# The gated MLP of a hybrid decoder block: convolution accumulated in PSUM, weight splits on GpSimd, token combinations made before the transposes

## The chip, the cores and the metric

The kernel runs on one core of one Trainium2 chip. The metric is the device time of one execution in microseconds (us). Engines are named TensorE (PE in the profile, PEld for its weight loads), VectorE (DVE), ScalarE (ACT), GpSimd (POOL) and SyncE (SP, which only issues DMAs here). The inputs and the output are float32, and so are all intermediate values.

## The reference

One decoder block on 1024 tokens of width 1024. Two groups of attention heads (stick-breaking and latent attention) share an input projection and an output projection; after that comes the part that the change touches, and a gated per-layer embedding at the end:

```python
x = x + rms_norm(mix, g_post_mix[i])

h = rms_norm(x, g_pre_ffn[i])
u = causal_depthwise_conv(h @ w_up[i], conv_w[i], conv_b[i])   # w_up: 1024 x 5632, three taps
gate, val = jnp.split(u, 2, axis=-1)
f = (jax.nn.gelu(gate, approximate=True) * val) @ w_down[i]    # w_down: 2816 x 1024
x = x + rms_norm(f, g_post_ffn[i])
```

## The kernel before

**Float32 by three products.** TensorE multiplies float32r operands. Each float32 value is split into a high part h (a rounding copy on ScalarE, line 97) and the rest l = value − h (one subtraction, line 98, on VectorE or, with `on_pool`, on GpSimd). A product is then three matmuls: h·h, h·l and l·h. The split's source can be in SBUF or, on VectorE, in PSUM.

**The up projection by seven block products.** The 1024 x 5632 product is made in 22 channel groups c of 128 gate and 128 value columns. For each, the 2 x 2 blocks are: token half (first, second 512 tokens), half of the 1024 inputs (k4), and gate or value (v). Instead of eight block products it makes seven, with sums of weight blocks and sums of token blocks. Two of the seven (`up_first`, lines 959 to 978) need only the first token half and run as filler inside the attention and the output projection; their results go to DRAM (`p1_dram`, `u_dram`). The other five need the token tiles t1 to t4 and b22, which are built from both halves (`combined`), and the weight sums s[0] to s[3] and one plain block (`up_sums`, `up_sum_4`, lines 925 to 935). Each of the five is twelve matmuls of 128x512 (`up_product`, lines 915, 917 and 922).

**The loop over channels** (from line 1221). For each c the five products t2, t1, t3, t4, b22 go into two PSUM banks, py and pz. py gathers t2, t3 and t4, and VectorE reads it after each of them (lines 1237, 1240, 1243); pz gathers t1 and b22 and is read at lines 1241 and 1245. The sums u of gate and value (128 channels x 1024 tokens) then go through `conv`: ScalarE writes y = w2·u + b (line 1215), VectorE adds two shifted terms in place (line 1217, y is in SBUF), ScalarE applies gelu to the gate's y (line 1247), VectorE multiplies it by the value's y (line 1248), and GpSimd's queue stores the product to `f_dram` (line 1249). Six PSUM banks go round for the products. The weights of the following products are made alongside: SP loads raw blocks (line 1205, five buffers, `WR`), GpSimd makes the four sums (lines 928, 929, 930, 934), ScalarE the high parts, and the low parts of two of the five splits are made by VectorE and of three by GpSimd. The split weights lie in a ring of eight slots.

**The token tiles.** `out_proj_mla` (from line 765) finishes the output projection of one token half: it normalises, adds x (line 798, on GpSimd), stores the sum, normalises again (line 805), and transposes 128 x 128 blocks (line 809). For the first half (th = 0) the transposed rows are split into `h2`. For the second half (th = 1) `combined` (from line 816) works on transposed tiles: it rebuilds the first half's values from h + l on GpSimd (line 832), copies one block out of PSUM (line 839), makes t1, t2, t3 on VectorE (lines 837, 841, 843) and t4 on GpSimd (line 849), and splits the five results, two of them on GpSimd.

**Order.** Each engine runs its instructions in a fixed order. The order is made when the program is built, from the order of the code, given priorities, and a simulated timeline; filler work is handed out by credits (`Fill.step`): `WO_RATE` is the credit per step of the output projection (first number) and per step marked "sums" or "chain" (second number). Buffers are taken in turn, and an instruction waits until the buffer's last reader is done. After the loop comes the down projection (`ffn_down`, line 1294), which needs four banks at a time and the same raw buffers `wr`.

Of the kernel before, what the change touches and what calls it, by code (L numbers as in the profile page):

```python
# [37 lines left out]
ML_RATE = (1.2, 0.8)  # L38
WO_RATE = (0.3, 2.5)
AHEAD = 0.9  # L40
EMB_RATE = 1.0

WR = 5
LATER = (500, 0, 0, 2000)
# [6 lines left out]
def tile_hybrid_block(ctx: ExitStack, tc: tile.TileContext, a: dict, out: bass.AP):  # L51
# [149 lines left out]
    def bank():  # L201
        return now["bank"]()
# [567 lines left out]
    def out_proj_mla(th, rows, h2):  # L770
# [21 lines left out]
        for j, t in enumerate(ts):  # L792
            dve.scalar_tensor_tensor(rows[j], rows[j], r[:, j:j + 1], g_post_mix, ALU.mult,
                                     ALU.mult)
            for h_ in hd_:
                xt = tmp()
                sp.dma_start(xt, a["x"][t * P:(t + 1) * P, h_])
                pool.tensor_tensor(rows[j][:, h_], rows[j][:, h_], xt, ALU.add)
            pool.dma_start(x1_dram[t], rows[j])
            yield "chain"  # L800
        r = rstd_rows()
        for j in range(4):
            for k4, h_ in enumerate(hd_):
                n = tmp()
                dve.scalar_tensor_tensor(n, rows[j][:, h_], r[:, j:j + 1], g_pre_ffn[:, h_],
                                         ALU.mult, ALU.mult)
                ps = bank() if th == 0 else one_bank(ptr, "tr")
                for k in range(4):
                    pe.transpose(ps[:, k * P:(k + 1) * P], n[:, k * P:(k + 1) * P], ident)
                if th == 0:  # L810
                    d = [z[:, k4 * 4:k4 * 4 + 4, j * P:(j + 1) * P] for z in h2]
                    split(d[0], d[1], ps.rearrange("p (k t) -> p k t", k=4))
                    yield "chain"
                elif k4 == 0:
                    ps0 = ps
                else:
                    yield from combined(j, ps0, ps, *h2)

    def combined(j, b12, b22, first, ts_):


        def out(i, src, on_pool=False):
            d = [z[:, :, j * P:(j + 1) * P] for z in ts_[i]]
            split(d[0], d[1], src.rearrange("p (k t) -> p k t", k=4), None, on_pool)

        def tmp2():
            return now["wo"].tile([P, H], F32, tag="wh", name=nm("t"), bufs=4)

        def raw(k4):
            t = tmp2()  # L830
            d = [z[:, k4 * 4:k4 * 4 + 4, j * P:(j + 1) * P] for z in first]
            pool.tensor_tensor(t.rearrange("p (k t) -> p k t", k=4), d[0], d[1], ALU.add)
            return t

        b11 = raw(0)
        t1 = tmp()
        dve.tensor_tensor(t1, b12, b11, ALU.subtract)
        s22 = tmp()
        act.copy(s22, b22)
        t2 = tmp()  # L840
        dve.tensor_tensor(t2, s22, t1, ALU.subtract)
        t3 = tmp2()
        dve.tensor_tensor(t3, s22, b12, ALU.subtract)
        out("t1", t1, True)
        yield "chain"
        out("t3", t3)
        b21 = raw(1)
        t4 = tmp2()
        pool.tensor_tensor(t4, b21, t2, ALU.subtract)
# [75 lines left out]
    def up_sums(raw, s):  # L925

        a21, a22, a11 = (raw(1, 0), raw(1, 1), raw(0, 0))
        pool.tensor_tensor(s[0], a21, a22, ALU.add)
        pool.tensor_tensor(s[1], s[0], a11, ALU.subtract)
        pool.tensor_tensor(s[2], a11, a21, ALU.subtract)  # L930
        return (s[1], False), (s[0], False), (s[2], True), (a22, True)

    def up_sum_4(raw, s1, dst):
        pool.tensor_tensor(dst, raw(0, 1), s1, ALU.subtract)
        return ((dst, True),)

    def first_up_sums():
# [14 lines left out]
        def splits(slots):  # L952
            last = sh.tile([P, H], F32, tag="uf", name=nm("uf"), bufs=3)
            res = []
            for src, on_pool in some + up_sum_4(raw, s[1], last):
# [24 lines left out]
    with tc.tile_pool(name="mla", bufs=1, side="right", reuse_waits="tile") as ml:  # L980
# [163 lines left out]
        for z in (make_k(0), make_q(0), make_k(1)):  # L1144
            for _ in z:
# [5 lines left out]
                 for n in range(16)]  # L1151
# [4 lines left out]
    y_cm[0].__exit__(None, None, None)  # L1156
    px = ctx.enter_context(tc.tile_pool(name="px3", bufs=2, space=PSUM, reuse_waits="tile"))
    py = ctx.enter_context(tc.tile_pool(name="py3", bufs=2, space=PSUM, side="right",
                                        reuse_waits="tile"))

# [9 lines left out]
    with tc.tile_pool(name="wo", bufs=1, side="right", reuse_waits="tile") as wo_:  # L1170
        now["wo"] = wo_
        rows1 = [sh.tile([P, D], F32, tag="s4", name=nm("row"), bufs=4) for _ in range(4)]
        for r in out_proj_sb(1, rows1):
            fill.step(WO_RATE[r in ("sums", "chain")])
        for r in out_proj_mla(1, rows1, (h2[0], tb)):
# [4 lines left out]
    now["bank"] = cycle([lambda: one_bank(px, "mm"), lambda: one_bank(py, "mm"),  # L1180
                         lambda: one_bank(pav, "av"), lambda: one_bank(px, "mm"),
                         lambda: one_bank(py, "mm"), lambda: one_bank(ppj, "pj")])
    shared.__exit__(None, None, None)
# [5 lines left out]

    def up_split(src, on_pool):  # L1190
# [9 lines left out]
    def up_weights():  # L1200

        for c in range(1, NCH):
            def raw(v, k4):
                t = up_tile("wr", 512, WR)
                sp.dma_start(t.rearrange("p (a b) -> p a b", a=4), up_block(v, c, k4))
                return t

            s = [up_tile("s", 512, 4) for _ in range(4)]
            for src, on_pool in up_sums(raw, s) + up_sum_4(raw, s[1], s[3]):
                yield up_split(src, on_pool)  # L1210

    def conv(v, c, u):
        y = up_tile(f"y{v}", S, 2)
        ci = v * NCH + c
# [8 lines left out]
    for c in range(NCH):  # L1223
# [22 lines left out]
        y = [conv(v, c, u[v]) for v in range(2)]  # L1246
        act.activation(y[0], y[0], AF.Gelu_apprx_tanh)  # L1247
        dve.tensor_tensor(y[0], y[0], y[1], ALU.mult)
        pool.dma_start(f_dram[c], y[0])
    tp_cm.__exit__(None, None, None)  # L1250
# [205 lines left out]
```

## Time and profile before

| | us |
|---|---|
| median of 3 runs | 1593.34 (1591.44 to 1596.71) |
| the profiled execution | 1593.64 |
| its span | 1591.5 |
| TensorE busy | 1434.4 (90%) |
| VectorE busy | 1164.3 (73%) |
| ScalarE busy | 831.4 (52%) |
| GpSimd busy | 607.6 (38%) |

A stage table has, for each stretch of time, the length and then for each engine the busy time and in brackets the number of instructions, then the clock granted to TensorE as a share of full speed, the busy share of the DMA engines, and the GB/s moved. A row of a line's view names line, engine, operation, what it writes and reads, the count, then the shortest, median and longest duration in ns, the first and the last start in us, and the shapes. A row of the waits has who waited, for whom, the total in us, the times, and the longest. A timeline row has start and duration in us, engine, line, operation and count, and in square brackets the idle time before it and what ended it.

### The profile page before, as it was taken

What the parts mean: (1) busy time and instruction counts of PE and PEld (TensorE: products, weight loads), DVE (VectorE), ACT (ScalarE), POOL (GpSimd) and SP (SyncE); (2) the same over time, 40 slices, a digit from 0 to 9 for tenths busy, and PEclk for the clock granted to TensorE, in tenths of its full rate; (3) what the DMA queues carried; (4) which work ended last, traced back from release to release, by engine and by line L of the source; (5) the groups of instructions that cost most, each with busy time, mean ns of one, the idle gap of its engine ahead of it and who ended that gap; (6) DMA issues with size and microseconds to landing.
All of it is one profiled execution on the core that took longest, in us unless ns stands there. A gap on an engine that the chain in (4) does not pass through costs nothing. (4 is left out here: it accounts for less than half of the span.)

```text
span 1591.5 us, 20521 instructions
## 1 busy us (share of the span) xinstructions
PE 1434.4 (90%) x6768; PEld 1169.9 (74%) x6768; DVE 1164.3 (73%) x1869; ACT 831.4 (52%) x1575; POOL 607.6 (38%) x548
## 2 busy tenths in 40 slices
PE   5997998987899888899987599989998999999996
PEld 4977886775688776778865487777767788888875
DVE  4569477999767778733567599999999654874697
ACT  6366455776778566645434343344344444654542
POOL 7107100011344325112365899889893000000033
PEclk9999999998999999999998799999999999999998
DMA  6031210122544433346654344444444766675354
GB/s 197 22 100 52 95 41 14 40 75 103 157 138 159 122 113 119 120 153 197 202 175 161 101 143 133 137 141 133 147 129 135 275 201 188 229 232 179 126 184 160
DMA packets 128570, 219.90 MB, mean 138 GB/s; under 512 B 13376, under 2 KB 50144, under 8 KB 128464
## 3 DMA queue, kind: packets, MB, share of 16 engines
q1 hardware_dynamic: 111920, 161.58, 32.9%
q0 software_dynamic: 16544, 57.01, 9.7%
q8 instruction: 53, 0.87, 0.2%
q14 instruction: 53, 0.43, 0.1%
HBM read 165.33 MB, written 53.22 MB: 137 GB/s over the span
## 5 line engine op out<-in xcount | busy, mean ns | idle before, releaser
L1217 DVE SCALAR_TENSOR_TENSOR y<-u,c_conv_w,y 128x1023 f32<-128x1023 f32 x88 | 162.8, 1852 | 9.3 <-ACT y L1215 9.2
L98 DVE TENSOR_TENSOR tl<-tr,th 128x512 fp32r<-128x512 f32 x192 | 103.2, 549 | 40.4 <-ACT th L97 35.1
L97 ACT CAST th<-tr 128x512 fp32r<-128x512 f32 x192 | 90.9, 485 | 53.8 <-PE tr L464 44.2
L98 DVE TENSOR_TENSOR wl<-ws,wh 128x512 fp32r<-128x512 f32 x73 | 63.5, 879 | 70.1 <-ACT wh L97 33.2
L464 PE MATMUL tr<-ident,w 128*128 128x128 f32 x576 | 103.2, 287 | 10.1 <-DVE tl L98 6.0
L98 DVE TENSOR_TENSOR f<-wr,f 128x512 fp32r<-128x512 f32 x88 | 60.7, 690 | 68.5 <-PE pj L122 34.3
L1215 ACT ACTIVATE y<-u,c_conv_b,c_conv_w 128x1024 f32<-128x1024 f32 x44 | 54.8, 1245 | 89.7 <-DVE u L1245 53.1
L1292 POOL DMA_DIRECT2D x_dram<-fd x8 | 4.3, 541 | 246.6 <-DVE fd L1291 235.0
L652 DVE TENSOR_TENSOR_SCAN kc<-kc,one_f 128x128 f32<-128x128 f32 (+3 forms) x64 | 88.0, 1381 | 13.0 <-ACT kc L649 12.9
L464 PEld LDWEIGHTS tr<-ident,w 128*128 128x128 f32 x576 | 74.4, 147 | 25.7 <-DVE tl L98 7.7
L479 PE MATMUL av<-tl,v 128*128 128x512 f32 x192 | 76.6, 400 | 18.4 <-DVE tl L98 17.9
L478 PE MATMUL av<-th,v 128*128 128x512 f32 x192 | 78.5, 409 | 13.4 <-ACT th L97 7.0
L98 POOL TENSOR_TENSOR ws<-s,ws 128x512 fp32r<-128x512 f32 x42 | 88.9, 2121 | 3.0 <-ACT ws L97 3.0
L97 ACT CAST f<-wr 128x512 fp32r<-128x512 f32 x88 | 54.5, 619 | 68.1 <-PE pj L121 30.5
L120 PE MATMUL mm<-wh,f 128*128 128x512 f32 x220 | 85.9, 393 | 0.0
L121 PE MATMUL mm<-wl,f 128*128 128x512 f32 x220 | 85.5, 391 | 0.0
L97 ACT CAST wh<-ws 128x512 fp32r<-128x512 f32 x76 | 46.7, 620 | 74.3 <-DMA ws<-in_w_up 27.8
L97 ACT CAST wh<-wr 128x512 fp32r<-128x512 f32 x88 | 54.6, 621 | 49.4 <-DMA wr<-in_w_down 35.7
L98 DVE TENSOR_TENSOR wl<-wr,wh 128x512 fp32r<-128x512 f32 x88 | 63.1, 717 | 19.1 <-ACT wh L97 19.0
L122 PE MATMUL mm<-wh,f 128*128 128x512 f32 x220 | 74.1, 393 | 0.0
L748 POOL TENSOR_TENSOR t<-t,t 128x512 fp32r<-128x512 f32 x32 | 41.2, 1289 | 84.1 <-ACT t L747 41.2
L1247 ACT ACTIVATE y<-y 128x1024 f32<-128x1024 f32 x22 | 23.4, 1062 | 85.5 <-DVE y L1217 85.5
(518 smaller groups left out, 4724.1 us busy)
## 6 DMA issues: line engine op xcount, KB each, us to landing
wr<-in_w_down SPq DMA_DIRECT2D x88, 256.0 KB, 3.0
wr<-f_dram SPq DMA_DIRECT2D x88, 256.0 KB, 2.9
wr<-in_w_up SPq DMA_DIRECT2D x84, 256.0 KB, 2.8
t<-o_dram SPq DMA_DIRECT2D x48, 256.0 KB, 3.1
ws<-in_w_up SPq DMA_DIRECT2D x47, 256.0 KB, 3.5
f_dram<-y POOLq DMA_DIRECT2D x22, 512.0 KB, 3.6
ws<-in_w_o SPq DMA_DIRECT2D x32, 256.0 KB, 3.1
ws<-in_w_in SPq DMA_DIRECT2D x24, 256.0 KB, 2.9
```

The lines of the kernel that those rows point to most:

```text
L97: act.copy(h, src)
L98: (pool if on_pool else dve).tensor_tensor(l, src, h, ALU.subtract)
L120: pe.matmul(ps, lh, rh, start=start, stop=False)
L121: pe.matmul(ps, lh, rl, start=False, stop=False)
L122: pe.matmul(ps, ll, rh, start=False, stop=stop)
L464: pe.transpose(tr[:, c:c + P], w[i][:, j * P:(j + 1) * P], ident)
L478: pe.matmul(av[:, lo:], v(j), th[:, lo:], start=j == 0, stop=False)
L479: pe.matmul(av[:, lo:], v(j), tl[:, lo:], start=False, stop=j == last)
L652: dve.tensor_tensor_scan(rev, rev, one_f[:, 0:1].to_broadcast([P, n]), 1.0, ALU.mult, ALU.mult)
L748: pool.tensor_tensor(ol, src, oh, ALU.subtract)
L1215: act.activation(y, u, AF.Identity, bias=conv_b[:, ci:ci + 1], scale=conv_w[:, ci, 2:3])
L1217: dve.scalar_tensor_tensor(y[:, d:], u[:, :S - d], conv_w[:, ci, 2 - d:3 - d], y[:, d:], ALU.mult, ALU.add)
```

## The change

Four things change in the code.

1. `conv` puts y into four PSUM banks (two tiles of two banks, one buffer each) and no longer into SBUF; gelu writes a new SBUF tile f, which is multiplied in place by the value's y and stored. The product banks fall from six to four: the pools px and py are closed before the loop and opened again after it.
2. In the loop all five splits run with `on_pool`, that is, their low part on GpSimd. The four sums stay as they are. The splits of the first channel (`first_up_sums`) all run on VectorE.
3. `combined` works on rows before the transposes. The first half's normalised rows are stored to `n0_dram` and loaded again; t1 to t4 are made on VectorE from rows in SBUF, and each of the five results is transposed into a PSUM bank and split from there, on ScalarE and VectorE. The addition of x for the second half moves from GpSimd to VectorE.
4. `WR` goes from 5 to 6, the second `WO_RATE` from 2.5 to 1.8, and the first four banks of the down projection are the four product banks.

```diff
-WO_RATE = (0.3, 2.5)
+WO_RATE = (0.3, 1.8)
...
-WR = 5
+WR = 6
...
+    n0_dram = [dram.tile([2, P, H], F32, name=f"n0_dram{j}") for j in range(4)]
...
-                pool.tensor_tensor(rows[j][:, h_], rows[j][:, h_], xt, ALU.add)
+                (pool, dve)[th].tensor_tensor(rows[j][:, h_], rows[j][:, h_], xt, ALU.add)
...
         for j in range(4):
+            ns = []
             for k4, h_ in enumerate(hd_):
                 n = tmp()
                 dve.scalar_tensor_tensor(n, rows[j][:, h_], r[:, j:j + 1], g_pre_ffn[:, h_],
                                          ALU.mult, ALU.mult)
...
+                ns.append(n)
                 if th == 0:
+                    pool.dma_start(n0_dram[j][k4], n)
+                    ps = bank()
+                    flip_split(ps, n, [z[:, k4 * 4:k4 * 4 + 4, j * P:(j + 1) * P] for z in h2])
                     yield "chain"
...
+            if th == 1:
+                yield from combined(j, ns, h2)
+
+    def flip_split(ps, n, d):
+
+        for k in range(4):
+            pe.transpose(ps[:, k * P:(k + 1) * P], n[:, k * P:(k + 1) * P], ident)
+        split(d[0], d[1], ps.rearrange("p (k t) -> p k t", k=4))
+
+    def combined(j, second, ts_):
...
+        b12, b22 = second
+        b11, b21 = tmp(), tmp()
+        sp.dma_start(b11, n0_dram[j][0])
+        sp.dma_start(b21, n0_dram[j][1])
+
+        def out(i, n):
+            flip_split(one_bank(ptr, "tr"), n, [z[:, :, j * P:(j + 1) * P] for z in ts_[i]])
+
+        out("b22", b22)
+        dve.tensor_tensor(b11, b12, b11, ALU.subtract)
+        yield "chain"
+        out("t1", b11)
         t2 = tmp()
-        dve.tensor_tensor(t2, s22, t1, ALU.subtract)
...
+        dve.tensor_tensor(t2, b22, b11, ALU.subtract)
         yield "chain"
...
         out("t2", t2)
-        out("b22", b22)
+        dve.tensor_tensor(b12, b22, b12, ALU.subtract)
         yield "chain"
-        out("t4", t4, True)
+        out("t3", b12)
+        dve.tensor_tensor(b21, b21, t2, ALU.subtract)
+        yield "chain"
+        out("t4", b21)
         yield "chain"
...
-        return (s[1], False), (s[0], False), (s[2], True), (a22, True)
+        return s[1], s[0], s[2], a22
...
-                split(w[0], w[1], src, None, on_pool)
+                split(w[0], w[1], src)
...
+    x_cm.__exit__(None, None, None)
+    y_cm.__exit__(None, None, None)
+    y_cm, py = psum("py4", 1, "right")
+    now["bank"] = cycle([lambda: one_bank(ptr, "tr"), lambda: one_bank(pav, "av"),
+                         lambda: one_bank(ptr, "tr"), lambda: one_bank(ppj, "pj")])
...
-        split(w[0], w[1], src, None, on_pool)
+        split(w[0], w[1], src, None, True)
...
-        y = up_tile(f"y{v}", S, 2)
+        y = py.tile([P, S], F32, tag=f"y{v}", name=nm(f"y{v}"))
...
-        act.activation(y[0], y[0], AF.Gelu_apprx_tanh)
-        dve.tensor_tensor(y[0], y[0], y[1], ALU.mult)
-        pool.dma_start(f_dram[c], y[0])
+        f = up_tile("f", S, 2)
+        act.activation(f, y[0], AF.Gelu_apprx_tanh)
+        dve.tensor_tensor(f, f, y[1], ALU.mult)
+        pool.dma_start(f_dram[c], f)
+    y_cm.__exit__(None, None, None)
...
-            banks = [bank() for _ in range(4)]
+            if th == dh == 0:
+                banks = [one_bank(p_, tag) for p_, tag in ((ptr, "tr"), (pav, "av"), (ptr, "tr"),
+                                                           (ppj, "pj"))]
+            else:
+                banks = [bank() for _ in range(4)]
```

More of the change, by code (lines that the diff above doesn't have):

```diff
@@ L813, in out_proj_mla @@
                     yield "chain"
[L814 to L839, printed above, removed]
+            if th == 1:
+                yield from combined(j, ns, h2)
@@ L954, in splits @@
             res = []
-            for src, on_pool in some + up_sum_4(raw, s[1], last):
+            for src in some + up_sum_4(raw, s[1], last):
                 w = [stage.tile([P, 512], F32R, tag=x, name=nm(x), bufs=4)
                      for x in ("wh", "wl")] if len(res) < 4 else [z[:, 0] for z in slots]
-                split(w[0], w[1], src, None, on_pool)
+                split(w[0], w[1], src)
                 res.append(w)
@@ L1156, in tile_hybrid_block @@
     y_cm[0].__exit__(None, None, None)
-    px = ctx.enter_context(tc.tile_pool(name="px3", bufs=2, space=PSUM, reuse_waits="tile"))
-    py = ctx.enter_context(tc.tile_pool(name="py3", bufs=2, space=PSUM, side="right",
-                                        reuse_waits="tile"))
+    x_cm, px = psum("px3", 2)
+    y_cm, py = psum("py3", 2, "right")
     now["bank"] = cycle([lambda: one_bank(py, "mm"), lambda: one_bank(pav, "av"),
@@ L1188, in tile_hybrid_block, with up_split @@
     turn = [1]
-    def up_split(src, on_pool):
+    def up_split(src):
         i = turn[0] % NK
@@ L1246, in tile_hybrid_block @@
         y = [conv(v, c, u[v]) for v in range(2)]
-        act.activation(y[0], y[0], AF.Gelu_apprx_tanh)
-        dve.tensor_tensor(y[0], y[0], y[1], ALU.mult)
-        pool.dma_start(f_dram[c], y[0])
+        f = up_tile("f", S, 2)
[3 more added lines that the diff above has]
+    y_cm.__exit__(None, None, None)
+    px = ctx.enter_context(tc.tile_pool(name="px5", bufs=2, space=PSUM, reuse_waits="tile"))
+    py = ctx.enter_context(tc.tile_pool(name="py5", bufs=2, space=PSUM, side="right",
+                                        reuse_waits="tile"))
+    now["bank"] = cycle([lambda: one_bank(px, "mm"), lambda: one_bank(py, "mm"),
+                         lambda: one_bank(pav, "av"), lambda: one_bank(px, "mm"),
+                         lambda: one_bank(py, "mm"), lambda: one_bank(ppj, "pj")])
     tp_cm.__exit__(None, None, None)
```

23 lines of the change are left out of this document (4 added, 19 removed).

## The prediction

> **What bounds the kernel now.** I read the stage table first, cut where the work changes: the end of the out projection with the token combinations, the loop over the 22 up-projection channels (steady part, then its last 22 us), and the down projection.
>
> ```profile
> core 0: us, PE busy (x) PEld busy (x) DVE busy (x) ACT busy (x) POOL busy (x), PEclk, DMA share, GB/s
> 814.00:902.00 88.00, 57.01 (x201) 42.24 (x201) 67.22 (x78) 35.40 (x64) 60.61 (x55) 0.78 0.42 140
> 902.00:1217.00 315.00, 292.64 (x1234) 230.93 (x1235) 289.35 (x245) 128.52 (x168) 282.01 (x165) 0.99 0.44 142
> 1217.00:1239.00 22.00, 20.11 (x89) 16.27 (x88) 19.17 (x23) 8.92 (x10) 3.60 (x7) 1.00 0.30 99
> 1239.00:1500.00 261.00, 259.82 (x1151) 213.01 (x1150) 162.08 (x326) 131.89 (x221) 3.96 (x8) 1.00 0.65 211
> ```
>
> The down projection is TensorE alone (259.82 of 261 us). In the loop, 902 to 1217, three engines look full. A channel has 60 matmuls, so 1234 are 20.6 channels and one takes 315 / 20.6 = 15.3 us; of that TensorE is busy 14.2, VectorE 14.0, GpSimd 13.7. What TensorE needs when nothing is late stands in the timeline: twelve matmuls from the first of one product to the first of the next.
>
> ```profile
> 1009.77 0.39 PE L915 MATMUL mm<-t2h,ws 128*128 128x512 f32 x1
> ...
> 1012.49 0.39 PE L915 MATMUL pj<-t1h,ws 128*128 128x512 f32 x1
> ```
>
> That is 2.72 us a product, 13.6 us a channel. The waits of TensorE in the same stretch say who takes the other 1.7 us (each restart is also slower than a running stream):
>
> ```profile
> PE mm L915 <- ACT ws L97: 9.9, 6, 3.3
> PE mm L915 <- DVE u L1241: 6.0, 8, 0.9
> PE pj L915 <- DVE u L1241: 4.6, 5, 0.9
> PE mm L915 <- DVE q L1240: 2.7, 5, 0.8
> PE av L915 <- DVE q L1240: 2.3, 3, 1.5
> ```
>
> VectorE reads a bank late (lines 1240, 1241), or a weight's split comes late; the first is VectorE's load, the second GpSimd's. Next: are their instructions as long as they must be? Minimum, median and maximum in ns, VectorE first, the L98 row for 920 to 1230 us:
>
> ```profile
> L1217 DVE SCALAR_TENSOR_TENSOR y<-u,c_conv_w,y x88: 1268/1722/4666, 916.7 to 1245.0; 128x1023 f32<-128x1023 f32 x44, 128x1022 f32<-128x1022 f32 x44
> L1248 DVE TENSOR_TENSOR y<-y,y x22: 1224/1226/2321, 928.3 to 1247.4; 128x1024 f32<-128x1024 f32 x22
> L1245 DVE TENSOR_TENSOR u<-q,mm x15: 673/675/681, 919.0 to 1240.6; 128x512 f32<-128x512 f32 x15
> L98 DVE TENSOR_TENSOR ws<-s,ws x38: 677/1193/1793, 926.3 to 1213.8; 128x512 fp32r<-128x512 f32 x38
> ```
>
> ```profile
> L928 POOL TENSOR_TENSOR s<-wr,wr x21: 1261/1287/2270, 899.9 to 1189.5; 128x512 f32<-128x512 f32 x21
> L934 POOL TENSOR_TENSOR s<-wr,s x21: 1294/2142/2282, 905.3 to 1200.8; 128x512 f32<-128x512 f32 x21
> L98 POOL TENSOR_TENSOR ws<-s,ws x40: 1297/2281/2305, 917.9 to 1215.7; 128x512 fp32r<-128x512 f32 x40
> L748 POOL TENSOR_TENSOR t<-t,t x32: 1257/1289/1312, 428.4 to 800.1; 128x512 fp32r<-128x512 f32 x32
> L1249 POOL DMA_DIRECT2D f_dram<-y x22: 531/556/567, 932.5 to 1249.0; - x22
> ```
>
> The pattern is plain. VectorE instructions with two SBUF inputs (1217, 98) stretch from 1.27 to 1.72 us and beyond; line 1245, with one input in PSUM, never does (673 to 681 ns), although GpSimd is busy nine tenths of the time. GpSimd's own 1.29 us becomes 2.3 in the loop, while in the attention stage (748) it stays at 1.29. The two engines hold each other up.
> The Trainium skill, "SBUF — State Buffer", section "Who interferes with whom", states that as a rule: a VectorE instruction with two SBUF inputs and a GpSimd instruction that reads SBUF exclude each other, and one with at most one SBUF input does not contend. The rows above agree. By that rule rival (d) below would have no chance; I leave it one, since no row here has VectorE writing PSUM.
>
> **The change, part by part.**
>
> *Convolution in PSUM.* The accumulator y moves to four PSUM banks, so line 1217 has one SBUF input (u), and the product f × y1 one too. No row shows a VectorE write into PSUM. Lower bound 1.23 us (the 1024-element product of line 1248, unstretched, 1224 ns), upper bound today's median 1.72. I take 1.28, just above the 1268 minimum: the 512-element pair of rows, 673 with PSUM and 677 without, shows no price for a PSUM read. VectorE per channel: 4 × 1.28 + 1.23 + 5 × 0.675 = 9.7 us against 14.0 (the two splits, medians 1193 ns, are gone as well); at the upper bound 11.5. Either is under 13.6.
>
> *All five splits on GpSimd.* The four sums (lines 928 to 934) stay there; nothing in the diff takes them away. Without contention 4 × 1.28 + 5 × 1.30 + 0.556 = 12.2 us per channel, 90% of 13.6. The words "no arithmetic ahead of them" fit only the token stage, where lines 832 and 849 go.
> A rule speaks against this: the Trainium skill, "GPSIMD Engine Reference", section "Engine selection", calls elementwise work on GpSimd about 2× slower than on VectorE. 1297 against 677 ns here agrees: the split is dearer where it goes. By the rule's factor it costs 2 × 0.677 = 1.35, and GpSimd's channel 12.5 in place of 12.2 us.
>
> *ScalarE* keeps its work: two y at 1.245, gelu 1.062, five copies at 0.609, 6.6 us a channel.
>
> ```profile
> L1215 ACT ACTIVATE y<-u,c_conv_b,c_conv_w 128x1024 f32<-128x1024 f32 x39 | 48.6, 1245 | 80.9 <-DVE u L1245 48.3 <-DVE u L1243 32.6
> L97 ACT CAST ws<-s 128x512 fp32r<-128x512 f32 x83 | 50.1, 609 | 19.5 <-POOL s L934 11.6 <-POOL s L929 5.3 <-POOL s L928 1.9
> ...
> L1247 ACT ACTIVATE y<-y x22: 1058/1062/1065, 927.2 to 1246.4; 128x1024 f32<-128x1024 f32 x22
> ```
>
> One y per half: y0 of the next channel waits for gelu, y1 for the product. That chain is 1.245 + 2 × 1.28 for each half, then 1.06 + 1.23: below 10 us of 13.6, so it is covered.
>
> *Four product banks in place of six.* A channel holds two (py, pz), so two channels are open, not three. Line 1240 must read py between t3 and t4; today t2 and t1 of the next channel, 5.4 us, stand between them. Two open channels allow the same order, so I cost it at nothing; what it costs without that cover is a rival.
>
> *The loop in sum.* I take 14.0 us a channel: 13.6 and 0.4 of waits (a quarter of today's 1.7, since VectorE falls from full to 71%). 1234 matmuls take 20.6 × 14.0 = 288 us: 27 saved; the 89 matmuls of the last 22 us save 1 more. Bounds: 36 saved at 13.6, 12 at GpSimd's worst (below).
>
> *Last channel.* Down-projection matmuls fill gaps at the end now; after the change only the banks that the last channels leave are free for them. This stall stands there even now:
>
> ```profile
> 1219.94 0.50 PE L915 MATMUL mm<-t4h,ws 128*128 128x512 f32 x1 [1.89 <-DVE q L1240]
> ```
>
> One or two of that size: +2 us (0 to 4).
>
> *Token combinations ahead of the transposes.* What ends this part now:
>
> ```profile
> 845.83 0.16 DVE L139 TENSOR_TENSOR rn<-rn,rn 128x4 f32<-128x4 f32 x1
> ...
> 895.12 1.30 POOL L98 TENSOR_TENSOR t4l<-t,t4h 128x512 fp32r<-128x512 f32 x1
> ...
> 896.45 1.75 SPq L1205 DMA_DIRECT2D wr<-in_w_up  x4
> ...
> 901.87 0.79 PE L915 MATMUL mm<-t1h,ws 128*128 128x512 f32 x1 [3.33 <-ACT ws L97]
> ```
>
> The last split of the last token frees the memory that the loop's weight tiles (wr) need; their load starts at once, and TensorE runs again 5.5 us later. So the end of the token work sets the loop's start. Four token tiles take 846 to 896, 12.6 us each. The unstretched prices:
>
> ```profile
> L805 DVE SCALAR_TENSOR_TENSOR t<-row,rn,g_pre_ffn x16: 721/746/3840, 623.3 to 882.9; 128x512 f32<-128x512 f32 x16
> L841 DVE TENSOR_TENSOR t<-t,t x4: 677/1778/5126, 852.6 to 888.8; 128x512 f32<-128x512 f32 x4
> L798 POOL TENSOR_TENSOR row<-row,t x16: 1279/1302/2276, 597.8 to 834.5; 128x512 f32<-128x512 f32 x16
> 850.85 1.03 PE L809 MATMUL tr<-ident,t 128*128 128x128 f32 x8
> ```
>
> After: VectorE per tile 2 × 0.75 + 4 × 0.68 + 5 × 0.68 = 7.6 us, with GpSimd silent, so nothing like the 5126 ns of line 841. GpSimd loses two sums, one difference and two splits. TensorE gets 12 more transposes a tile, 48 × 0.13 = 6 us, in a stretch where it is idle 31 of 88 us. The eight residual additions move from GpSimd (1.30) to VectorE (0.68): +5.4 us there, while the chain to row 4 gets shorter. Each flip is a chain of its own (transposes, copy, split; about 2 us), with two banks, and each tile waits for two loads from n0_dram. Best case, VectorE bound: 30 us of tiles, 18 us gained. Worst: +6, below. I take 9.5 to 11 us a tile, −6 us. The eight stores of n0 (0.556 us each on GpSimd's queue) fall into the attention stage, where this token half is filler (line 805 first runs at 623.3):
>
> ```profile
> 600.00:700.00 100.00, 86.66 (x471) 70.59 (x471) 68.04 (x120) 60.96 (x119) 27.70 (x33) 0.97 0.39 127
> ```
>
> GpSimd, fifth, is busy 28 us of 100 there, so I cost them at nothing, 4.4 us if exposed. The two WO_RATE credits, 16 × 2.5 = 40 and 24 × 1.8 = 43, hand out the same filler; WR = 6 adds a load buffer in stages that TensorE or VectorE bound: nothing.
>
> **Sum.** The profiled execution took 1593.64 us (span 1591.5 and 2.1 around it), 0.3 above the median of the runs, 1593.34. 1593.6 − 28 + 2 − 6 = **1562 us**.
>
> **Rivals.**
> (a) *GpSimd becomes the bound.* It is at 12.2 of 13.6 us with an in-order queue. Today it waits (315 − 282) / 20.6 = 1.6 us a channel, for copies and for the store of f behind line 1248. If that grows to 2.5, a channel is 14.7, the loop saves 12, total 1594 − 12 − 4 = 1578. For it: 90% load. Against: VectorE, for which most of it waits, has room.
> (b) *The loads of n0 come late.* They queue on SP, where a prefetch blocks today:
>
> ```profile
> SPq L108 <- POOL uf L934: 25.9, 1, 25.9
> ```
>
> ```profile
> 849.05 29.41 SPq L108 DMA_DIRECT2D ws<-in_w_ple_gate  x3
> ```
>
> Three prefetches, up to 878 us, in the token loop. With the last two tiles' loads behind such a wait the token work ends some 6 us later than now: 1594 − 28 + 2 + 6 = 1574.
> (c) *Slower: with four banks TensorE runs the channels one after the other.* Then t4 follows t3 and waits for line 1240: 0.675 and a restart, 0.8 us, plus 1.28 for each convolution step ahead of it on VectorE: 2.1 with one, 3.4 with two. It decides from 1.9 us a channel on (today's 1.7 and the 4 us from the other parts). With one 1598, with two 13.6 + 3.4 = 17.0, loop +35, 1624; between them 1611. Against: the order needs only two open channels.
> (d) *The change doesn't do what it says: PSUM frees nothing.* Then GpSimd's instructions keep today's mean, (13.7 − 0.556) / 7 = 1.88 us, and nine with the store take 17.5 us a channel: loop +45, total 1594 + 45 − 4 = 1635. Against: line 1245.
>
> **How the numbers follow.** Forecast 0.61, its own range 1543 (13.6 us a channel, 14 us from the tokens) to 1574; (a) 0.14; (b) 0.12; (c) 0.08; (d) 0.05. The range 1543 to 1590 takes in (a) and (b), and leaves out (c), (d) and a little below. A change under 0.3% can't be told from none: the runs before spread by that. Faster (under 1588.6): 0.60 + 0.12 + 0.11 + 0.02 = 0.85. Same: 0.01 + 0.02 + 0.01 + 0.02 = 0.06. Slower: 0.04 + 0.05 = 0.09.
>
> **What would show it.** Line of the convolution at 1.25 to 1.3 us with minimum and median together: PSUM frees the pair; a spread to 2 us is (d). GpSimd's sums and splits all near 1.29 and its busy time 12.2 us a channel. Twelve-matmul steps of 2.72 us with channels 13.6 to 14.3 us apart; TensorE waiting for the copies of weights is (a), for the q line before every t4 (c). The first wr load at about 890 us instead of 896.45; if loads of n0 stand last in the waits there, (b). I am wrong if the channel stays above 15 us, or if a stage outside 800 to 1250 moves by more than 5 us.

## The result and the profile after

| | us |
|---|---|
| before, median of 4 runs beside it | 1594.4 (1591.44 to 1596.71) |
| after, median of 4 runs | 1547.34 (1542.91 to 1552.33) |
| ratio | 0.9707, 95% interval 0.9671 to 0.9742 |
| the profiled execution of after | 1542.91, span 1541.1 |

The changed kernel is 47 us (2.9%) faster. The profiled execution is the fastest of its four, 4.4 us under the median; that matters below.

The stage table of the kernel after, cut at the end of the token work (887), near the loop's last channels (1190) and where the down projection runs alone (1239); columns as before.

```profile
core 0: us, PE busy (x) PEld busy (x) DVE busy (x) ACT busy (x) POOL busy (x), PEclk, DMA share, GB/s
814.00:887.00 73.00, 60.69 (x273) 47.04 (x272) 53.72 (x93) 35.15 (x63) 13.90 (x23) 0.91 0.66 227
887.00:1190.00 303.00, 302.33 (x1332) 249.49 (x1330) 206.89 (x225) 140.92 (x179) 252.19 (x213) 1.00 0.47 153
1190.00:1239.00 49.00, 48.57 (x212) 39.29 (x211) 26.90 (x41) 22.34 (x37) 0.54 (x1) 1.00 0.77 265
1239.00:1500.00 261.00, 259.93 (x1163) 213.24 (x1162) 176.90 (x418) 130.66 (x228) 21.15 (x26) 1.00 0.58 188
```

The loop is now a TensorE stage: 302.33 us busy of 303, where it was 292.64 of 315. VectorE fell from 92% to 68%, GpSimd stands at 83%. What is left of idle TensorE in this part lies ahead of the loop, in the 73 us of token work.

The waits in the loop after, 902 to 1190 us, TensorE's whole list and then the largest of GpSimd's: who waited, for whom, total us, times, longest.

```profile
PE tr L911 <- DVE q L1237: 0.7, 1, 0.7
```

```profile
POOL f_dram L1247 <- DVE f L1246: 29.5, 10, 11.5
POOL ws L99 <- PE tr L918: 7.9, 10, 1.2
```

TensorE waits once in 21 channels. The relation to GpSimd has turned over: GpSimd makes the splits so early that it waits for TensorE to give a ring slot back (line 99 behind 918). Its 29.5 us at the store (1247) harm nobody.

The instructions of the loop after, minimum, median and maximum in ns. (Line 1214 is the old 1217, 99 the old 98, 926 and 930 the old 930 and 934.)

```profile
L1214 DVE SCALAR_TENSOR_TENSOR y<-u,c_conv_w,y x88: 1272/1282/1291, 900.0 to 1192.4; 128x1023 f32<-128x1023 f32 x44, 128x1022 f32<-128x1022 f32 x44
L1246 DVE TENSOR_TENSOR f<-f,y x22: 1217/1221/1223, 908.6 to 1195.3; 128x1024 f32<-128x1024 f32 x22
L926 POOL TENSOR_TENSOR s<-wr,wr x20: 1279/1302/1332, 898.9 to 1150.7; 128x512 f32<-128x512 f32 x20
L930 POOL TENSOR_TENSOR s<-wr,s x20: 1280/1306/1326, 901.4 to 1152.0; 128x512 f32<-128x512 f32 x20
L99 POOL TENSOR_TENSOR ws<-s,ws x80: 1293/1317/1751, 900.1 to 1161.3; 128x512 fp32r<-128x512 f32 x80
L1247 POOL DMA_DIRECT2D f_dram<-f x22: 533/557/568, 911.4 to 1196.9; - x22
```

The convolution step has 1272, 1282 and 1291 where it had 1268, 1722 and 4666, and the sums and splits of GpSimd stand at 1.3 us where they went to 2.3. In the median, neither engine holds the other up any more.

To say where the 50 us between the two profiles came from, I mark four places by the first and last starts in the views of single tiles: line 793 (794 after), the first scaled row; line 805 (807), the first row of the first token tile; the last split of t4 (for before in the prediction, 895.12); and the matmuls of b22, which close each channel. Before, then after:

```profile
L793 DVE SCALAR_TENSOR_TENSOR row<-row,rn,g_post_mix x4: 1278/1790/2299, 819.4 to 824.0; 128x1024 f32<-128x1024 f32 x4
L805 DVE SCALAR_TENSOR_TENSOR t<-row,rn,g_pre_ffn x8: 739/1252/3840, 846.1 to 882.9; 128x512 f32<-128x512 f32 x8
L915 PE MATMUL mm<-b22h,ws x60: 387/393/501, 914.5 to 1237.6; 128*128 128x512 f32 x60
L922 PE MATMUL mm<-b22h,ws x60: 388/389/395, 916.4 to 1238.7; 128*128 128x512 f32 x60
```

```profile
L794 DVE SCALAR_TENSOR_TENSOR row<-row,rn,g_post_mix x4: 1280/1282/1285, 814.9 to 818.5; 128x1024 f32<-128x1024 f32 x4
L807 DVE SCALAR_TENSOR_TENSOR t<-row,rn,g_pre_ffn x8: 737/744/753, 835.4 to 870.0; 128x512 f32<-128x512 f32 x8
L99 DVE TENSOR_TENSOR t4l<-tr,t4h x4: 676/692/692, 856.6 to 885.7; 128x512 fp32r<-128x512 f32 x4
L911 PE MATMUL av<-b22h,ws x44: 389/389/397, 897.9 to 1173.1; 128*128 128x512 f32 x44
L918 PE MATMUL pj<-b22h,ws x44: 388/389/389, 917.9 to 1185.2; 128*128 128x512 f32 x44
```

| stretch | before | after | difference, us |
|---|---|---|---|
| up to the first scaled row | 819.4 | 814.9 | −4.5 |
| scaled row to first token tile | 26.7 | 20.5 | −6.2 |
| the four token tiles, to the end of the last split | 50.3 | 51.0 | +0.7 |
| to the first channel's b22 | 18.1 | 11.5 | −6.6 |
| first b22 to last b22 | 324.2 | 287.3 | −36.9 |
| last b22 to the end of the span | 352.8 | 355.9 | +3.1 |
| sum | 1591.5 | 1541.1 | −50.4 |

The first row can't be put down to the change. In the variants below, the first scaled row lies anywhere between 814.2 and 825.2 us with the new token part and between 817.9 and 820.4 with the old one, so that 4.5 us are within what single executions differ by; and this execution is 4.4 us under its median. The last row belongs to the loop: before, the down projection's first matmuls are woven into the last channels from 1217.7 on, 21 us ahead of the last b22; after, from 1177.2 on, 8 us ahead: 24 of them before the last b22 is closed, against 12, so that more are left for later. So the loop itself gave 34 to 37 us, the token part and the first channel about 12.

### The profile page after: what moved, and what is told of

It reads as the page before. It is cut to its first block, busy times and chain, and to the rows that moved or that the text cites. A ratio compares the mean times of both kernels' runs of the same rounds, so it can differ in the third digit from the quotient of the medians.

```text
span 1541.1 us, 20717 instructions
## 1 busy us (share of the span) xinstructions
PE 1421.4 (92%) x6816; PEld 1169.5 (76%) x6816; DVE 1047.6 (68%) x1850; ACT 832.2 (54%) x1571; POOL 532.5 (35%) x567
## 4 chain that ended last, share of the span: by engine, by line
PE 63%; DVE 13%; DMA 9%; issue 7%; ACT 5%; POOL 3%; SPq 0%; DVEq 0%; ACTq 0%; POOLq 0%
PE tr L911 4%; PE tr L913 4%; PE tr L918 4%; PE pj L121 4%; PE pj L122 4%; PE pj L123 4%; PE mm L122 3%; PE mm L121 3%; PE mm L123 3%; PE pj L911 2%; DMA ws<-in_w_up 2%; PE pj L913 2%; PE pj L918 2%; DMA t<-o_dram 2%; PE tr L465 2%
## 5 line engine op out<-in xcount | busy, mean ns | idle before, releaser
L1214 DVE SCALAR_TENSOR_TENSOR y<-u,c_conv_w,y 128x1023 f32<-128x1023 f32 (+1 forms) x88 | 112.5, 1283 | 25.6 <-ACT y L1212 24.4
L99 POOL TENSOR_TENSOR ws<-s,ws 128x512 fp32r<-128x512 f32 x84 | 110.3, 1320 | 13.1 <-PE tr L918 6.7
L99 DVE TENSOR_TENSOR wl<-ws,wh 128x512 fp32r<-128x512 f32 x73 | 55.9, 773 | 70.2 <-ACT wh L98 42.3
L479 PE MATMUL av<-th,v 128*128 128x512 f32 x192 | 79.1, 412 | 13.6 <-ACT th L98 6.8
L98 ACT CAST ws<-s 128x512 fp32r<-128x512 f32 x84 | 51.2, 613 | 52.0 <-PE tr L913 33.2
L121 PE MATMUL mm<-wh,f 128*128 128x512 f32 x176 | 69.0, 392 | 0.0
L122 PE MATMUL mm<-wl,f 128*128 128x512 f32 x176 | 68.9, 391 | 0.0
L121 PE MATMUL pj<-hTh,wh 128*128 128x512 f32 x160 | 65.3, 408 | 0.0
```

The lines of the kernel that those rows point to most:

```text
L98: act.copy(h, src)
L99: (pool if on_pool else dve).tensor_tensor(l, src, h, ALU.subtract)
L121: pe.matmul(ps, lh, rh, start=start, stop=False)
L122: pe.matmul(ps, lh, rl, start=False, stop=False)
L479: pe.matmul(av[:, lo:], v(j), th[:, lo:], start=j == 0, stop=False)
L1214: dve.scalar_tensor_tensor(y[:, d:], u[:, :S - d], conv_w[:, ci, 2 - d:3 - d], y[:, d:], ALU.mult, ALU.add)
```

## The experiments

Eleven variants, in the order in which they were run. Times are medians; the kernel before ran beside each call at 1593 to 1596 us. The marks of the profiles, in us, for all of them:

| kernel | first token tile | last t4 split starts | first b22 | last b22 | first to last | median time |
|---|---|---|---|---|---|---|
| before | 846.1 | 895.1 | 914.5 | 1238.7 | 324.2 | 1594.4 |
| after | 835.4 | 885.7 | 897.9 | 1185.2 | 287.3 | 1547.3 |
| e1 convolution in PSUM alone | 846.2 | 894.1 | 908.6 | 1194.1 | 285.5 | 1557.0 |
| e2 five splits on GpSimd alone | 847.2 | 894.9 | 913.6 | 1265.2 | 351.6 | 1626.3 |
| e3 token part alone | 833.9 | 885.4 | 898.2 | 1225.3 | 327.1 | 1586.8 |
| e4 after, two splits on VectorE | 840.1 | 890.4 | 903.5 | 1188.9 | 285.4 | 1544.5 |
| e5 after, old credit | 844.3 | 889.5 | 901.6 | 1189.0 | 287.4 | 1545.6 |
| e6 after, x added on GpSimd | 843.6 | 892.6 | 904.7 | 1192.0 | 287.3 | 1551.7 |
| e7 after, t4 in other memory | 837.6 | 886.7 | 899.7 | 1185.2 | 285.5 | 1545.7 |
| e8 before, four product banks | 844.9 | 892.6 | 912.3 | 1244.2 | 331.9 | 1607.1 |
| e9 after, four banks for transposes | 840.5 | 877.8 | 892.4 | 1179.7 | 287.3 | 1540.2 |
| e11 e9 with two splits on VectorE | 840.4 | 879.2 | 894.7 | 1180.2 | 285.5 | 1539.0 |
| e12 e9 with five raw buffers | 837.4 | 874.8 | 890.9 | 1178.2 | 287.3 | 1539.1 |

The first three take the change apart.

### e1: the convolution in PSUM alone

```diff
-        y = up_tile(f"y{v}", S, 2)
+        y = py.tile([P, S], F32, tag=f"y{v}", name=nm(f"y{v}"))
```

with the banks it needs (four for the products, as in the change) and the new tile f; two splits stay on VectorE, the token part is the old one.

> The kernel before with the convolution in PSUM, four product banks and nothing else of the change: two of five splits stay on VectorE, the token work is the old one. Theory (the SBUF pair is what the loop lacked): lines with y run at 1.28 us, VectorE has 4 x 1.28 + 1.23 + 5 x 0.68 + 2 x 0.7 to 1.2 = 11.1 to 12.1 us a channel, GpSimd 7 x 1.3 to 1.6 + 0.56 = 9.7 to 11.8, so channels come 13.6 to 13.9 us apart and the kernel takes 1560 to 1570. Rival (it is the moved splits that relieve VectorE): channels stay near 15 us, 1590 or more.

Measured: 1556.98 us, ratio 0.976 (0.9731 to 0.9788). The stage table of this kernel for 940 to 1180 us, and its convolution step:

```profile
940.00:1180.00 240.00, 240.00 (x1061) 198.72 (x1060) 193.97 (x217) 112.30 (x144) 159.20 (x134) 1.00 0.48 157
```

```profile
L1218 DVE SCALAR_TENSOR_TENSOR y<-u,c_conv_w,y x88: 1273/1282/1291, 911.8 to 1201.2; 128x1023 f32<-128x1023 f32 x44, 128x1022 f32<-128x1022 f32 x44
```

TensorE is busy all of 240 us, and a channel takes 285.5 / 21 = 13.6 us. This part alone gives 2.4 of the 2.9%, with the splits where they were. The time lies 3 us below the expected 1560 to 1570.

### e2: all five splits on GpSimd alone

```diff
-        split(w[0], w[1], src, None, on_pool)
+        split(w[0], w[1], src, None, True)
```

The convolution stays in SBUF.

> The kernel before with all five splits on GpSimd, the convolution still in SBUF. Theory: VectorE's convolution keeps its two SBUF inputs, GpSimd's instructions keep a mean near 1.88 us, nine and the store are 17.5 us a channel and GpSimd sets the pace: loop 30 to 45 us longer, 1620 to 1640. Rival (moving the splits is what helps): VectorE falls to 11.5 us a channel, 1560 to 1575.

Measured: 1626.34 us, ratio 1.0181 (1.0155 to 1.0207): slower. The same stretch, the waits of TensorE in it, and the two lines in contention:

```profile
940.00:1180.00 240.00, 213.33 (x891) 172.24 (x890) 178.78 (x149) 91.42 (x117) 234.43 (x146) 0.96 0.38 127
```

```profile
PE mm L922 <- POOL ws L98: 13.4, 4, 4.6
PE mm L915 <- DVE q L1240: 6.0, 1, 6.0
PE pj L922 <- POOL ws L98: 4.7, 3, 2.3
PE mm L915 <- ACT ws L97: 2.6, 2, 1.7
```

```profile
L1217 DVE SCALAR_TENSOR_TENSOR y<-u,c_conv_w,y x88: 1270/1715/7970, 915.8 to 1272.4; 128x1023 f32<-128x1023 f32 x44, 128x1022 f32<-128x1022 f32 x44
L98 POOL TENSOR_TENSOR ws<-s,ws x84: 1272/1332/2356, 905.1 to 1243.7; 128x512 fp32r<-128x512 f32 x84
```

GpSimd is busy 234 of 240 us and TensorE waits for its splits: this is what the prediction's rival (a) looks like. A channel takes 240 / 891 × 60 = 16.2 us where 17.5 were expected, and the loop is 27 us longer than before, just under the expected 30 to 45. The move of the splits is a loss by itself.

### e3: the token part alone

The rows of `combined`, n0, the addition of x on VectorE and the credit 1.8, in the kernel before; loop, banks, splits and the five raw buffers stay.

> The kernel before with the token part alone (rows stored and loaded again, combinations on VectorE ahead of the transposes, the addition of x on VectorE, WO_RATE 1.8); loop as before. Theory (parts add): the first store of f comes 12 to 17 us earlier, the channels stay 15.1 us apart, 1577 to 1583. Rival (the earlier start is lost in a loop that VectorE and GpSimd bound, or gains only with the idle GpSimd of the new loop): 1588 to 1596.

Measured: 1586.79 us, ratio 0.9948 (0.9925 to 0.9972). In the profile, which is of the fastest of seven executions, the token work ends ten us earlier and the loop starts as in after (898.2); the loop itself is no shorter than before (327.1 against 324.2). The time lies between the two expected ranges: the first store of f does come 15.5 us earlier (917.0 in place of 932.5), but of the 16.3 us by which the first b22 is ahead, 2.9 are lost again in the loop and 2.8 behind it. In medians the shares add up, 2.4% of e1 and 0.5% of e3 being the 2.9% of the whole change, though the interval of e3 alone goes from 0.3 to 0.75%.

### e4: the change, with two splits back on VectorE

```diff
+        on_pool = (turn[0] - 1) % 5 > 1
...
-        split(w[0], w[1], src, None, True)
+        split(w[0], w[1], src, None, on_pool)
```

> The changed kernel with the first two splits of each channel back on VectorE. Theory: TensorE stays the bound, 13.6 us a channel, no difference beyond 4 us (1543 to 1552). Rival (GpSimd alone must do them): splits with two SBUF inputs hold GpSimd up again, channels above 14.2 us, 1560 or more.

Measured: 1544.48 us, ratio 0.9676 (0.9655 to 0.9697); the interval overlaps that of after.

```profile
940.00:1180.00 240.00, 240.00 (x1060) 198.75 (x1059) 194.00 (x216) 111.71 (x143) 157.43 (x133) 1.00 0.48 156
```

Against after, VectorE is busy 25 us more in this stretch (194.0, 169.2) and GpSimd 40 us less (157.4, 197.0), and TensorE is at 240.00 of 240 in both. Once y is in PSUM, it makes no difference that can be measured here who makes these splits.

### e5: the change, with the old credit

`WO_RATE = (0.3, 2.5)`.

> The changed kernel with the second WO_RATE back at 2.5. 24 steps then hand out 60 pieces of filler in place of 43. Theory: the filler (first-half up projection) ends some 12 us earlier in the token stage, TensorE idles there longer, and the loop starts no earlier: 0 to 8 us slower than the changed kernel, 1547 to 1555. Rival (the credit is noise, as the prediction had it): within 2 us of it.

Measured: 1545.61 us, ratio 0.9689 (0.9663 to 0.9716): no difference from after that these runs can tell, as the rival had it. The marks of this profile say little: it is the slowest execution of its five, that of after the fastest of its four. Its first scaled row is already ten us later (825.2, 814.9), and its four tiles take 45.9 us in place of 51.0. That the filler only changes its place is likely, but not shown.

### e6: the change, with the addition of x on GpSimd

```diff
-                (pool, dve)[th].tensor_tensor(rows[j][:, h_], rows[j][:, h_], xt, ALU.add)
+                pool.tensor_tensor(rows[j][:, h_], rows[j][:, h_], xt, ALU.add)
```

> The changed kernel with the addition of x for the second token half back on GpSimd. Theory: from the first scaled row to the first token tile it takes 26 us in place of 20.5, as before the change, and the loop starts 4 to 7 us later: 1551 to 1555. Rival (the token chain has slack there): within 2 us of the changed kernel.

Measured: 1551.7 us, ratio 0.9735 (0.971 to 0.976), 4.4 us above after, though the intervals overlap. The two marks of the token part in this kernel:

```profile
L794 DVE SCALAR_TENSOR_TENSOR row<-row,rn,g_post_mix x4: 1279/1790/2318, 814.4 to 819.0; 128x1024 f32<-128x1024 f32 x4
L807 DVE SCALAR_TENSOR_TENSOR t<-row,rn,g_pre_ffn x8: 741/744/751, 843.6 to 875.4; 128x512 f32<-128x512 f32 x8
```

With GpSimd's additions back, the scaled rows stretch again (1790 in place of 1282 ns), and from them to the first tile it takes 29.2 us in place of 20.5 (26 were expected). The token work ends 6.9 us later than in after and the first b22 comes 6.8 us later: here the end of the token work does set the loop's start, one for one. In e9 below it is less: the token work ends 7.9 us earlier there, the first b22 comes 5.5 us earlier.

### e7: the change, with t4 in another buffer

```diff
-        dve.tensor_tensor(b21, b21, t2, ALU.subtract)
+        t4 = now["wo"].tile([P, H], F32, tag="wh", name=nm("t"), bufs=4)
+        dve.tensor_tensor(t4, b21, t2, ALU.subtract)
```

> The changed kernel with t4 written to a tile of the pool wo, where the kernel before had its token tiles; the loop's raw weight tiles take over that memory. Theory: their first load waits for the transposes of the last t4, about 885 us in place of 873, TensorE waits 3 to 6 us for the second channel's weights: 1549 to 1554. Rival (the early load is worth nothing, the copies of ScalarE set the start): within 2 us of the changed kernel.

Measured: 1545.73 us, ratio 0.9696 (0.9671 to 0.9721). The raw loads of the loop still start at 872.5 us (873.0 in after), so the edit didn't bring about the late load that it was made for. The time is the one that the rival expected, but as the edit missed its aim, it decides nothing.

### e8: the kernel before, with four product banks

```diff
-    now["bank"] = cycle([lambda: one_bank(px, "mm"), lambda: one_bank(py, "mm"),
-                         lambda: one_bank(pav, "av"), lambda: one_bank(px, "mm"),
-                         lambda: one_bank(py, "mm"), lambda: one_bank(ppj, "pj")])
+    now["bank"] = cycle([lambda: one_bank(px, "mm"), lambda: one_bank(pav, "av"),
+                         lambda: one_bank(px, "mm"), lambda: one_bank(ppj, "pj")])
```

for the loop alone.

> The kernel before with four product banks in the loop in place of six, nothing else. Theory: two open channels are enough, the order of products stays, channels 15.0 to 15.3 us apart: 1590 to 1599. Rival (four banks put t4 right behind t3): 0.8 to 3.4 us a channel more, 1605 to 1640.

Measured: 1607.07 us, ratio 1.0086 (1.006 to 1.0112): 12.7 us slower, where 1590 to 1599 was expected. It lies in the range of the rival, but not by the rival's way: the products follow each other in the same order as before, with t2 and t1 between t3 and t4. TensorE's waits in this kernel, 940 to 1180 us:

```profile
PE av L915 <- DVE u L1244: 13.7, 8, 1.7
PE mm L915 <- DVE q L1239: 7.4, 7, 1.1
PE av L915 <- DVE u L1240: 7.1, 8, 0.9
```

The first wait is new. (Lines 1239, 1240 and 1244 are lines 1240, 1241 and 1245 of before.) A product bank comes back only after VectorE has read it for b22, and with two open channels that reading is what the next but one channel's t1 waits for. The longest of these waits shows why VectorE is late there: a stretched convolution step of 4.69 us stands ahead of the reading.

```profile
1010.46 4.69 DVE L1216 SCALAR_TENSOR_TENSOR y<-u,c_conv_w,y 128x1023 f32<-128x1023 f32 x1 [0.19 <-ACT y L1214]
1015.07 0.67 DVE L1244 TENSOR_TENSOR u<-q,av 128x512 f32<-128x512 f32 x1
1015.89 0.47 PE L915 MATMUL av<-t1h,ws 128*128 128x512 f32 x1 [1.71 <-DVE u L1244]
```

Between the two profiles, 14.1 us apart, the loop starts 2.2 us earlier, takes 7.7 longer from the first to the last b22, and 8.6 more lie behind it, where TensorE waits once for 5.0 us at the start of the down projection. Four banks do cost something, as long as VectorE is late.

### e9, e11 and e12: four banks for the transposes

The stage ahead of the loop was what TensorE still idled in. Its largest waits after, 835 to 902 us:

```profile
PE tr L821 <- DVE t3l L99: 3.5, 2, 3.3
PE tr L821 <- DVE t2l L99: 2.1, 1, 2.1
PE tr L821 <- DVE b22l L99: 0.8, 1, 0.8
PE mm L911 <- ACT wh L98: 0.7, 1, 0.7
PE tr L821 <- DVE t4l L99: 0.4, 1, 0.4
```

The transposes of one result (821) wait for the split of an earlier one, which still reads their bank. So e9 gives them four banks in turn:

```diff
+    turns = cycle([lambda: one_bank(ptr, "tr"), lambda: one_bank(pav, "av"),
+                   lambda: one_bank(ptr, "tr"), lambda: one_bank(ppj, "pj")])
...
-            flip_split(one_bank(ptr, "tr"), n, [z[:, :, j * P:(j + 1) * P] for z in ts_[i]])
+            flip_split(turns(), n, [z[:, :, j * P:(j + 1) * P] for z in ts_[i]])
```

> The changed kernel with one edit: the transposes of the five token results take turns over four PSUM banks instead of two. My theory: with two banks the transposes wait for the split that still reads the bank (3.5 us in two waits of TensorE for VectorE's split in the token stage, the longest 3.3), and with GpSimd out of this stage the two banks and the tmp buffers are what keeps a token tile at 12.7 us where VectorE's own work is 7.6. Then the four token tiles, 51.0 us from the first tile's row to the last split, should fall to 42 to 47, and the time by 3 to 8 us, to about 1540 us. Rival: the tiles wait for the normalised rows, their loads or the four tmp buffers, and the loop's start hangs on the first channel's weights; then the time stays at 1547 (within 2 us).

e11 is e9 with the two splits of e4 on VectorE:

> The same, and two of the five weight splits back on VectorE as before the change. With the convolution in PSUM the place of these two splits made no difference of its own (1544.5 against 1547.3, intervals overlapping), so the theory expects the time of the run with four banks alone, within 3 us. Rival: GpSimd's queue, at 12 us of 13.6 a channel, delays the first channels' weights after the token work; then this version is 3 to 5 us below the one with four banks alone.

e12 is e9 with `WR = 5`:

> The version with four banks for the transposes, with five raw weight buffers instead of six (WR 5). The prediction costed the sixth buffer at nothing because TensorE or VectorE bounds the stages that use it. Theory: in the loop TensorE is busy all the time, the raw blocks come ahead of need, and the time stays at 1540 us (within 3 us). Rival: now that GpSimd's sums run at 1.29 us and the loop follows TensorE, the load ahead matters, in the loop's start or in the down projection, which uses the same buffers; then 4 us or more above 1540.

Measured: e9 1540.19 us, ratio 0.9656 (0.9638 to 0.9674); e11 1538.96, 0.9655 (0.9636 to 0.9674); e12 1539.11, 0.9653 (0.9629 to 0.9678). TensorE's waits in e9, 835 to 902 us, and the stage ahead of the loop:

```profile
PE pj L821 <- DVE b22l L99: 1.6, 1, 1.6
PE mm L914 <- ACT wh L98: 1.5, 1, 1.5
```

```profile
814.00:887.00 73.00, 66.25 (x320) 53.00 (x320) 56.24 (x104) 38.45 (x70) 24.03 (x33) 1.00 0.76 263
```

The four token tiles take 840.5 to 878.5, 38 us in place of 51.0 (my estimate was 42 to 47), the loop starts earlier, and the time falls by 7 us against after. The intervals of after and e9 touch (0.9671 and 0.9674), so the size is less certain than the sign: e9, e11 and e12 share the edit, and every run of theirs (up to 1542.19 us) is below the fastest of after. These three beat both kernels. Between them there is nothing to choose: the place of two splits and the sixth raw buffer are worth nothing that can be measured.

## Why the prediction was right, and where

Forecast 1562 (1543 to 1590), measured 1547: on the forecast's side and inside its range, near the low end. It was short by some 15 us, and the terms say where: some 9 in the loop (36.9 us in place of 28), some 6 ahead of the first channel's last product (12 in place of 6).

**Convolution in PSUM, 1.28 us: right to the digit.** 1282 ns median, and no spread. VectorE's 9.7 us a channel: 4 × 1.282 + 1.221 + 5 × 0.675 = 9.7. Rival (d), that PSUM frees nothing, is gone; e1 shows the gain with nothing else changed but the banks and the tile f that go with it; no run separates these, but the convolution step has the durations of after there. The Trainium skill's "SBUF — State Buffer", section "Who interferes with whom", gives the rule for it, and the trace of after agrees: with one SBUF input on VectorE, GpSimd's instructions are at 1.30 us beside it.

**Nine GpSimd operations a channel, 12.2 us: right, and so was taking it for no bound.** With the medians above, 4 × 1.30 + 5 × 1.317 + 0.557 = 12.3. It runs ahead of TensorE all the same. (The prediction's 12.5 us, with splits at 1.35, is 12.4 when summed again.) But part of the credit is misplaced: of VectorE the prediction counts that "the two splits (...) are gone as well" as a part of its relief. e4 shows that this move is worth nothing once y is in PSUM, and e2 that without that it costs some 30 us (1626.3 against 1595.7 beside it). Rival (a) is seen in e2 alone.

**Loop, 14.0 us a channel, −28: mis-sized.** The step that failed is "0.4 of waits (a quarter of today's 1.7)". TensorE waited 0.7 us in all, and the loop went to the bound that the prediction gave for 13.6 us a channel, 36 us. I had scaled the waits with VectorE's load, although the largest of them (9.9 us in total, for line 97) was for weights, whose copies wait for GpSimd's sums. They didn't scale: with neither engine stretched they went to nothing, in e1 too, where TensorE is busy all of 240 us.

**Four banks "at nothing": right for this kernel, for a reason that I gave too little weight.** e8 costs 12.7 us; between the profiles 7.7 of 14.1 us are in the loop. Rival (c) was right that four banks can cost something, but the condition that I set, the order of the products, isn't what it hangs on: no order changed. (Its price of 1598 to 1624 us was for the changed kernel, so that e8's 1607 doesn't bear it out.) It hangs on VectorE reading in time, which its stretched steps prevent in e8; in the changed kernel, where they are gone, it does. So e1's gain is a net one: the bank cost is inside it, paid off by the room on VectorE.

**Last channel, +2: not there as a stall.** In the last part of the loop TensorE waits 0.4 us in place of 1.9. What the table shows, +3.1, is work of the down projection that no longer fits into gaps.

**Token part, −6: right in size by luck, wrong in its parts.** "9.5 to 11 us a tile" failed: 51.0 / 4 = 12.7. (Its sums don't quite close either: 9.5 to 11 us a tile would be 6 to 12 us gained, and 30 us of tiles 20, not 18.) What was late next is what the prediction had listed and not priced, the flips with two banks; e9 shows it, with 38 / 4 = 9.5. The 6 us came ahead of the tiles, where GpSimd's additions had stretched VectorE's rows (e6) and where the prediction had put a cost, +5.4 on VectorE, beside a shorter chain that it didn't price. The first channel gave another 6.6, which stood in no term.

**The mark "first wr load at about 890": wrong.** It came at 873.0, before the token work ended, and it does so in e1 (877.4) and e3 (872.3) as well, each of which has half of the change. Before, that load waited 8.1 us for the last t4 split. What the early load is worth can be read from e1, whose token work is the old one: the wait of 3.33 us for a copied weight block, which the prediction shows at 901.87, is gone (it stands at 3.7 and 3.6 us in e2 and e8), and from the end of the last split to the first b22 it takes 13.2 us in place of 18.1. The same stretch takes 17.4 and 18.4 us in e2 and e8, where the load comes as late as before, and 11.4 to 15.4 in every kernel where it comes early. So most of the 6.6 us of the first channel goes with the early load; why it comes early is another question. That the new places of the tiles in memory cut this wait is likely, but e7, made for it, didn't test it; it stays open. That the end of the token work sets the loop's start holds by e6, but no longer by the raw loads, which is the path that the prediction drew; that it now goes through the products' own operands is argued, not shown.

**Loads of n0, rival (b): a small part of it happened.** Not behind a prefetch, but behind their own buffer; a row of SP's wait list of after, 700 to 910 us, and two steps of the chain that ended last:

```profile
SPq L830 <- PE tr L821: 15.5, 3, 7.9
```

```profile
860.45 2.74 DMA t<-n_dram
...
870.72 2.64 DMA t<-n_dram
```

The load can't be issued before the transposes have read the buffer, and about 2.7 us stand on the chain ahead of each of the last two tiles.

**The credits, the sixth buffer: nothing that can be measured, as costed** (e5, and e12 in the kernel of e9). **Outside 800 to 1250 us** nothing moved by more than 5 us.

## What to carry to other kernels

When two engines stretch each other's instructions, look first for an operand that can live in PSUM: here moving one accumulator gained 2.4%, while moving work between the same two engines gained nothing with it and lost 1.8% without it. Cost PSUM banks by what the engine that reads them has to spare, and not by their count alone: here two banks fewer cost 12.7 us with a busy, stretched VectorE, and left TensorE without a wait with one that had room. And after a gain, look at the stage ahead: the two transpose banks, which the change gave five results a token tile to carry in place of two, were the next 7 us.

## What the runs showed of the hardware that I had not expected

- A median hides how contention falls. In the loop before, GpSimd's splits had a median of 2281 ns and VectorE's steps 1722. In e2, with GpSimd busy 98%, the median of its splits is 1332, but their mean between 940 and 1180 us is still 1696 (2170 before), and its sums have medians of 1.3 to 2.2 us. VectorE's median stays at 1715, its mean is 1.82 us (1.96 before), and its longest step goes from 4666 to 7970 ns. So the pair still hold each other up in e2, with the load moved, if less on GpSimd's side than before.
- Accumulating in place in PSUM costs VectorE next to nothing: 1282 ns against 1268 for the shortest in SBUF. For ScalarE it is a little cheaper to write y there, 1210 ns against 1245 in the median, and gelu that reads it there takes 1028 against 1062:

```profile
L1212 ACT ACTIVATE y<-u,c_conv_b,c_conv_w x44: 1191/1210/1213, 898.8 to 1186.4; 128x1024 f32<-128x1024 f32 x44
L1245 ACT ACTIVATE f<-y x22: 1019/1028/1033, 907.6 to 1194.3; 128x1024 f32<-128x1024 f32 x22
```

- The loop's length with two splits on VectorE is 285.4 or 285.5 us in all three such kernels with y in PSUM (e1, e4, e11) and 287.3 or 287.4 in five with all splits on GpSimd; e7 is the exception, 285.5. No median shows this difference.
